# The scan of a two-layer hybrid backbone: the triangular inverse in whole steps, decay products on 64 rows each, copies on other engines

## The chip, the cores and the metric

The kernel runs on one core of a Trainium2 chip, as one program. The metric is device microseconds of one execution; before the change three executions took 2302.88, 2305.74 and 2308.2 us, median 2305.74.

The core has a TensorE (matmuls; "PE", with weight loads as "PEld"), VectorE ("DVE"), ScalarE ("ACT"), GpSimd ("POOL") and SyncE ("SP", which here issues nearly all DMAs). Each engine works through its own instructions in the order in which the program holds them, and waits on semaphores for the others.

## The reference

Two layers on 512 latent tokens and 256 context tokens of 1024 features, in float32: attention and a SwiGLU feed-forward, then a bidirectional RWKV-7 mixer and another feed-forward. The change touches only the mixer's scan, for 16 heads of 64 features in both directions:

```python
decay = exp(-exp(-softplus(-(w0[d] + tanh(xw @ w1[d]) @ w2[d])) - 0.5))
a     = sigmoid(a0[d] + (xa @ a1[d]) @ a2[d])
k_d   = k * (1 + (a - 1) * k_a)
...
def step(S, inp):                  # one token
    w_t, k_t, v_t, kk_t, a_t = inp[:5]
    sa = einsum('bhvk,bhk->bhv', S, -kk_t)
    S = S * w_t + sa[..., None] * (kk_t * a_t) + v_t[..., None] * k_t
    y = einsum('bhvk,bhk->bhv', S, r_t)
```

The scan runs over the context first, then over the latents, forwards for d = 0 and backwards for d = 1; the two y are added. The rank-64 matrices `rwkv_w2` and `rwkv_a2` (2 directions, 64 by 1024) give decays and rates.

## The kernel before

**The scan in chunks.** The kernel takes 64 tokens (a chunk) at a time. Inside a chunk the recurrence becomes a unit triangular system, whose inverse is worked out once; between chunks only the state S is carried. A *stage* is a pass p (the context, then the latents in two halves) over eight heads g of both directions, four chunks each. There are six stages. What stage s + 1 needs is made while stage s runs: four feature tiles by `elem` (with `front` for the next tile), then one `invert`.

**`front` (L1014 to L1036)** loads a tile's `kk` and the weights `wa` (L1022, four DMAs of 64 by 128), multiplies them with `t1` and `ta` (the tanh and linear inner products of both directions, 64 rows each, so 128 partitions hold both) and applies tanh on ScalarE (L1029, L1030), a scaling on GpSimd (L1033) and a running sum on VectorE (L1035). `wa` is one buffer of [128, 2, 2, 128], zeroed once: direction d fills its own 64 rows of `wa[:, d, x]`, the other 64 stay zero, and the product at L1028 runs over all 128 rows. Its result `z` (one bank, tag "z") is for one direction at a time.

**`elem` (L1038 to L1117)** makes from that the decayed keys and queries (`BK` at L1078 and L1079, `AR` and `GA`, for latents `R` at L1083), the bonus (L1084 to L1093), and the products inside the chunks (L1102 to L1107), which ScalarE copies into `GA` (masked by GpSimd, L1111) and into `AB`, the blocks to be inverted (L1115, L1116).

**`invert` (L1120 to L1181)** inverts 128 unit triangular blocks of 32 by 32, one on a partition, by forward substitution on VectorE: after a 32 by 32 transpose (L1123) and a mask (L1124, GpSimd), step s (1 to 30) adds to the rows below s, n = 31 - s of them, the multiple E[row, s] of row s, m = s columns. For m up to 3 (L1132) and n up to 3 (L1137) it goes by single fused instructions. For the 24 steps between, the rows are split into two halves: the outer product of either half (L1144, into `tmp`, a part of `O2`), then the sum of either half (L1147). Two transposes follow (L1150, L1151), TensorE merges pairs of blocks (L1162, L1176, L1178; results in a bank of tag "mg"), and ScalarE and VectorE copy the parts to `Xs` (L1168 on VectorE: the upper left blocks; L1169, L1181 on ScalarE).

**`scan` (L1211 to L1288)**, four chunks of a stage: S is the decayed state (L1226, VectorE); its halves are copied into `Tt` (L1227 on ScalarE, L1228 on VectorE, from the upper to the lower 64 partitions); `Bt` is a transpose (L1234, L1235); for latents `Rb` is filled from `R`, of either head by four copies (L1240: h = 0 on VectorE, h = 1 on ScalarE), and multiplied and masked into `GR` (L1244, L1245). Then come the products `pp` (L1252), copied to `Pb` (L1253 ScalarE, L1254 VectorE), `pu` with the inverse (L1258), copied to `Tt` (L1260, L1261), `pn` (L1267) and the new state `Sn` (L1272), and for latents `py` (L1281, L1282).

**The order of the work.** A planner sets it when the program is built: it takes each engine's instructions by the order of the program text as a priority, as soon as its own model has their inputs and buffers ready. The result is a fixed list for each engine. In the text a stage's `scan` stands first, then the next stage's four `elem`, then `invert`. Beside the first tiles run the products for v (L1197 to L1199), beside the context's stages those for r (L1308).

Of the kernel before, what the change touches and what calls it, by code (L numbers as in the profile page):

```python
# [10 lines left out]
F32 = mybir.dt.float32  # L11
# [6 lines left out]
P = 128  # L18
# [4 lines left out]
T = L + C  # L23
# [14 lines left out]
def tile_hybrid_backbone(ctx: ExitStack, tc: tile.TileContext, a: dict, out: bass.AP, dbg=None, stop=None, start=None):  # L38
# [32 lines left out]
    # ---- parameters, feature by feature on the partitions  # L71
# [44 lines left out]
    # ---- adaLN modulation: one block of 512 columns of mod_w  # L116
# [34 lines left out]
    # ---- the activation table of a function, loaded once x is there and before the function's first use  # L151
# [3 lines left out]
    # ---- 1 / sqrt(sum / n + eps), refined by a Newton step  # L155
# [11 lines left out]
    # ---- the sum of squares of the tokens sl, partition by partition, but for the last feature tile, whose squares follow  # L167
# [13 lines left out]
    # ---- the reciprocal root mean squares of nt tiles of tokens, tokens on the partitions  # L181
# [9 lines left out]
    # ---- the same on every partition, of the tokens dg has room for  # L191
# [7 lines left out]
    # ---- scale and shift of normed tokens  # L199
# [8 lines left out]
    # ---- a block of weights [nk * 128, cols], as the exact sum of two float32r parts  # L208
# [13 lines left out]
    # ---- out[f, t] += sum_d W[d, f] X[d, t] in three float32r passes; of several products all at once, step by step  # L222
# [10 lines left out]
    # ---- 512 columns of weights, as the exact sum of two float32r parts  # L233
# [19 lines left out]
    # ---- a product added to xT by its streams' gates  # L253
# [9 lines left out]
    # ---- xT += gate * (W^T X); the last tiles by halves of the tokens  # L263
# [23 lines left out]
    # The gate and up products of a pair of feature tiles by Winograd's form of Strassen's seven: the weights  # L287
    # A (features, d) and the tokens B (d, tokens) in 2 x 2 blocks,
    #   S1 = A21 + A22, S2 = S1 - A11, S3 = A11 - A21, S4 = A12 - S2
    #   T1 = B12 - B11, T2 = B22 - T1, T3 = B22 - B12, T4 = B21 - T2  # L290
    #   P1 = A11 B11, P2 = A12 B21, P3 = S4 B22, P4 = A22 T4, P5 = S1 T1, P6 = S2 T2, P7 = S3 T3
    #   C11 = P1 + P2, C12 = P1 + P6 + P5 + P3, C21 = P1 + P6 + P7 + P4, C22 = P1 + P6 + P7 + P5
    # Every sum is float32, every product three float32r passes.
    ORDER = (1, 2, 5, 6, 7, 3, 4)

    # ---- modulated norm of xT, in its place, as the blocks B11, B21, B22, T1 .. T4, each the exact sum of two float32r parts
# [51 lines left out]
    # ---- SwiGLU of the normed blocks, gated into xT; the hidden features in pairs of tiles  # L348
# [112 lines left out]
    # ================= x and ctx, features on the partitions  # L461
# [30 lines left out]
    # ---- layer 1's modulated norm of a stream, in its place  # L492
# [14 lines left out]
    # ================= layer 0: attention  # L507
    def layer0():
        at = ExitStack()
        with ExitStack() as qs:  # L510
# [43 lines left out]
            # rotary tables with the gains folded in; a head's features as (half, axis, pair)  # L554
# [27 lines left out]
            # heads' features onto the partitions; a pair of token tiles behind the products  # L582
# [151 lines left out]
        # ================= layer 0: projection and feed-forward  # L734
# [44 lines left out]
    # ================= layer 1: the RWKV mixer  # L779
# [7 lines left out]
    with ExitStack() as rw:  # L787
# [37 lines left out]
        with ExitStack() as de:  # L825
# [17 lines left out]
            # neighbours' sum, and the first lerp of it  # L843
# [57 lines left out]
            # the latents' second half again before their first, so that either pass reads one run  # L901
# [14 lines left out]
            # of a feature tile its heads, and the heads' features again from the two parts of a value  # L916
# [63 lines left out]
        # The scan's passes: the context, then the latents in two halves (each direction starts at its own  # L980
        # end). A stage is a pass over eight heads of both directions, 4 chunks of 64 tokens each. What a
        # stage needs of decays, keys and queries is worked out beside the stage before it.
# [10 lines left out]
        was = [tm.tile([P, 2, 2, P], F32, name=f"wa{z}") for z in range(1)]  # L993
        for z in Xss + was + ARs:
            nc.gpsimd.memset(z, 0.0)
# [7 lines left out]
        # a tile's decays begin before what is left of the tile before it  # L1003
# [10 lines left out]
        def front(p, f):  # L1014
# [4 lines left out]
            wa = was[0]  # L1019
            for x, nm_ in enumerate(("rwkv_w2", "rwkv_a2")):  # L1020
                for d in range(2):
                    nc.sync.dma_start(out=wa[hid(d), d, x], in_=a[nm_][0, d, :, P * f:P * f + P])  # L1022
            lw = tm.tile([P, 2, 256], F32, name="lw", tag="lw", bufs=2)
            at = tm.tile([P, 2, 256], F32, name="at", tag="at", bufs=2)
            for d in range(2):
                z = pE.tile([P, 2, 256], F32, name="z", tag="z")
                for x, src in enumerate((t1, ta)):
                    nc.tensor.matmul(z[:, x], wa[:, d, x], src[:, T0(p, d):T0(p, d) + 256], start=True, stop=True)  # L1028
                nc.scalar.activation(lw[:, d], z[:, 0], AF.Tanh, bias=hw0[:, d, f:f + 1], scale=0.5)  # L1029
                nc.scalar.activation(at[:, d], z[:, 1], AF.Tanh, bias=ha0[:, d, f:f + 1], scale=-0.5)  # L1030
# [7 lines left out]
        def elem(p, f):  # L1038
# [55 lines left out]
            # the products within the chunks; of the reverse direction's own the transposes  # L1094
# [24 lines left out]
        # unit triangular inverses, 128 blocks of 32 x 32 at a time, one on a partition, then merged in pairs  # L1119
        def invert():  # L1120
# [6 lines left out]
            tmp = O2.rearrange("p i b -> p (i b)")[:, 0:256]  # L1127
            for s in range(1, 31):
# [11 lines left out]
                h = (n + 1) // 2  # L1140
                parts = ((s + 1, s + 1 + h, 0), (s + 1 + h, 32, h * m))
                tvs = [tmp[:, o:o + (b - a_) * m].rearrange("p (a b) -> p a b", b=m) for a_, b, o in parts]
                for (a_, b, _), tv in zip(parts, tvs):
                    nc.vector.tensor_tensor(out=tv, in0=E[:, a_:b, s:s + 1].to_broadcast([P, b - a_, m]),  # L1144
                                            in1=E[:, s:s + 1, :s].to_broadcast([P, b - a_, m]), op=ALU.mult)
                for (a_, b, _), tv in zip(parts, tvs):
                    nc.vector.tensor_tensor(out=E[:, a_:b, :s], in0=E[:, a_:b, :s], in1=tv, op=ALU.add)  # L1147
# [18 lines left out]
            for h in range(2):  # L1166
                for d, o in ((0, o1), (1, o2)):
                    nc.vector.tensor_copy(Xs[lo(h), :, d, :, 0:32], o[lo(h), :, d])  # L1168
                    nc.scalar.copy(Xs[hi(h), :, d, :, 32:64], o[hi(h), :, d])  # L1169
# [13 lines left out]
        # beside v, tokens on the partitions  # L1183
# [27 lines left out]
        def scan(p, g):  # L1211
            fs = [f_tiles[p, 4 * g + q] for q in range(4)]
            Xs = Xss[0]
            for i in range(4):
# [6 lines left out]
                if not first:  # L1221
# [6 lines left out]
                    nc.vector.tensor_copy(Tt[HS[0], :, :, 1], S[HS[1]])  # L1228
# [7 lines left out]
                if p:  # L1236
                    GR = slot_pool["B"].tile([P, 2, 4, 2, 64], F32, name="GR", tag="GR")
                    for f in range(4):
                        for h in range(2):
                            (nc.scalar.copy if h else nc.vector.tensor_copy)(slot_pool["Rb"][HS[h], h, :, f], fs[f][2][HS[h], i:8 - i:7 - 2 * i, :])  # L1240
# [49 lines left out]
        # beside the context's passes  # L1290
# [40 lines left out]
    # ================= layer 1: readout, projection and feed-forward of the latents, final norm  # L1331
# [134 lines left out]
```

## Time and profile before

| | |
|---|---|
| median of three runs | 2305.74 us |
| span of the profiled execution | 2302.6 us |
| scan, from the first `front` to the end of the last stage | about 1253 to 1826 us of the span |
| first inverse begins | 1314.7 us |
| last inverse's transposes end | 1765.1 us |

The profile is one execution. Engine rows give busy microseconds. In a row of a group stand line, engine, operation, output <- inputs, partitions x elements and the count; behind the first bar the busy time and the mean of one in ns, behind the second the idle time of the engine just before them and what ended it. In a row of one line or tile the three numbers are minimum, median and maximum in ns. In a timeline row stand the start, the length, the engine and the line; "x2" is two neighbours merged. A window's row has the window, its length, then busy time and count for PE, PEld, DVE, ACT and POOL, the granted share of TensorE's clock, the DMA engines' share and GB/s. The chain of waits is followed back from the last instruction; its "by line" gives shares of the window.

### The profile page before, as it was taken

The numbers are of one execution on the slowest core, as the hardware profiler recorded it, in microseconds if no ns is written. First come the engines' busy times: TensorE is split into PE (matmuls) and PEld (weight loads), VectorE is DVE, ScalarE is ACT, GpSimd is POOL, SyncE is SP. The second block draws the span as 40 slices with busy tenths as digits, with TensorE's granted clock in tenths as the row PEclk, the third lists the DMA queues.
The fourth block names the chain that finished last, engine by engine and source line by source line (L and its number), as shares of the span: only waits on it lengthen the run. The fifth ranks groups of instructions, "written<-read, shape, count | busy, mean of one in ns | idle before, by whom it ended". The sixth has DMA issues, their size and how long they took to land.

```text
span 2302.6 us, 42745 instructions
## 1 busy us (share of the span) xinstructions
PE 2034.6 (88%) x16422; PEld 1779.6 (77%) x16422; DVE 1669.9 (73%) x3382; ACT 1094.9 (48%) x2276; POOL 790.8 (34%) x663
## 2 busy tenths in 40 slices
PE   6999999797999999995988978767888777899998
PEld 4995555586999999994767956656777666899998
DVE  4565556449877777768465597798888758988896
ACT  5446656434333333335343764765664534444443
POOL 1110000027434443423142531552430325666661
PEclk7999999998999999997988979778889987999999
DMA  8206660421321222111326543432321631433332
GB/s 298 67 25 222 237 237 21 148 91 48 109 74 63 74 68 74 62 55 64 100 88 211 148 121 120 121 107 64 110 62 54 189 121 47 138 97 97 105 97 74
DMA packets 178714, 247.94 MB, mean 108 GB/s; under 512 B 16808, under 2 KB 109968, under 8 KB 178128
## 3 DMA queue, kind: packets, MB, share of 16 engines
q1 hardware_dynamic: 177792, 244.37, 33.0%
q8 instruction: 130, 2.13, 0.4%
q10 hardware_dynamic: 352, 0.60, 0.1%
q0 software_dynamic: 368, 0.26, 0.1%
q14 instruction: 72, 0.59, 0.1%
HBM read 199.04 MB, written 33.55 MB: 101 GB/s over the span
## 4 chain that ended last, share of the span: by engine, by line
PE 63%; DVE 20%; ACT 5%; issue 5%; DMA 4%; POOL 2%; SPq 1%; DVEq 0%; ACTq 0%; POOLq 0%
PE yps L429 13%; PE A L395 8%; PE C L395 5%; PE B L395 5%; PE yps L228 5%; PE po L724 3%; DVE O L1144 3%; PE pj L228 3%; PE S L705 2%; DVE E L1147 2%; PE PTp L719 2%; PE mps L126 2%; DVE wu L241 2%; PE qps L578 2%; PE qps L580 2%
## 5 line engine op out<-in xcount | busy, mean ns | idle before, releaser
L429 PE MATMUL yps<-gh,wu 128*128 128x384 f32 (+2 forms) x1120 | 323.4, 345 | 3.7 <-DVE xT L258 3.6
L258 DVE SCALAR_TENSOR_TENSOR xT<-yps,modT,xT 128x384 f32<-128x384 f32 (+2 forms) x348 | 183.9, 548 | 134.1 <-PE yps L429 95.0
L241 POOL TENSOR_TENSOR wu<-wr,wu 128x512 fp32r<-128x512 f32 x77 | 107.1, 1392 | 472.6 <-ACT wu L239 456.9
L239 ACT CAST wu<-wr 128x512 fp32r<-128x512 f32 x252 | 154.6, 620 | 222.2 <-PE A L395 66.4
L429 PEld LDWEIGHTS yps<-gh,wu 128*128 128x128 f32 x1120 | 201.6, 188 | 16.5 <-DVE xT L258 4.7
L239 ACT CAST wu<-ws 128x512 fp32r<-128x512 f32 x176 | 108.0, 620 | 200.2 <-PE yps L429 86.5
L241 DVE TENSOR_TENSOR wu<-wr,wu 128x512 fp32r<-128x512 f32 x175 | 157.7, 903 | 50.8 <-ACT wu L239 47.8
L429 PE MATMUL yps<-gl,wu 128*128 128x384 f32 (+2 forms) x560 | 192.1, 344 | 0.0
L360 POOL TENSOR_TENSOR ws<-wr 128x512 f32<-128x512 f32 x88 | 130.1, 1482 | 165.8 <-DMA wr<-in_ffn_wg_dram 71.5
L241 DVE TENSOR_TENSOR wu<-ws,wu 128x512 fp32r<-128x512 f32 x111 | 125.8, 1139 | 9.8 <-ACT wu L239 9.8
L241 POOL TENSOR_TENSOR wu<-ws,wu 128x512 fp32r<-128x512 f32 x65 | 88.1, 1356 | 90.3 <-ACT wu L239 87.6
L429 PEld LDWEIGHTS yps<-gl,wu 128*128 128x128 f32 x560 | 105.4, 188 | 4.5
L228 PE MATMUL yps<-oTh,wu 128*128 128x512 f32 (+2 forms) x416 | 101.6, 347 | 8.2 <-ACT wu L239 8.2
L708 DVE TENSOR_REDUCE mx<-S 128x1 f32<-128x768 f32 (+1 forms) x96 | 74.7, 778 | 44.4 <-PE S L705 43.7
L720 ACT COPY PT<-PTp 128x384 f32<-128x384 f32 (+1 forms) x160 | 69.3, 465 | 54.0 <-PE PTp L719 53.8
L395 PE MATMUL C<-x5h,wu 128*128 128x384 f32 (+1 forms) x352 | 85.6, 318 | 6.0 <-ACT x5h L329 5.2
L719 PEld LDWEIGHTS PTp<-ident,pr 128*128 128x128 f32 x448 | 50.2, 144 | 50.5 <-issue 23.6
L395 PE MATMUL A<-x1h,wu 128*128 128x384 f32 (+1 forms) x352 | 88.0, 315 | 1.1 <-ACT x1h L329 1.1
L395 PE MATMUL B<-x2h,wu 128*128 128x384 f32 (+1 forms) x352 | 83.8, 310 | 4.7 <-ACT x2h L329 4.6
L1147 DVE TENSOR_TENSOR E<-E,O 128x110 f32<-128x110 f32 (+22 forms) x288 | 84.2, 325 | 0.3
L395 PE MATMUL A<-x6h,wu 128*128 128x384 f32 (+1 forms) x352 | 83.1, 314 | 1.0 <-DVE wu L241 1.0
L1144 DVE TENSOR_TENSOR O<-E 128x110 f32<-128x110 f32 (+22 forms) x288 | 82.4, 322 | 1.9
(408 smaller groups left out, 6365.4 us busy)
## 6 DMA issues: line engine op xcount, KB each, us to landing
mw<-in_mod_w_dram SPq DMA_DIRECT2D x48, 1024.0 KB, 5.3
wr<-in_ffn_wg_dram SPq DMA_DIRECT2D x44, 512.0 KB, 3.8
wr<-in_ffn_wu_dram SPq DMA_DIRECT2D x44, 512.0 KB, 3.6
wr<-in_ffn_wd_dram SPq DMA_DIRECT2D x44, 512.0 KB, 3.9
wraw<-in_rwkv_wrkv_dram SPq DMA_DIRECT2D x32, 256.0 KB, 3.1
wraw<-in_attn_wqkv_dram SPq DMA_DIRECT2D x12, 512.0 KB, 4.5
xT<-xd SPq DMA_DIRECT2D x2, 3072.0 KB, 9.8
AR<-lw SPq DMA_DIRECT2D x48, 128.0 KB, 2.3
```

Of the source, the lines that this page charges most:

```text
L228: nc.tensor.matmul(ps, w(k), x(k, sl), start=(k == 0 and i == 0), stop=(k == nk - 1 and i == 2))
L239: nc.scalar.copy(hi, raw)
L241: (nc.gpsimd if lane["n"] % 3 == 0 else nc.vector).tensor_tensor(out=lo, in0=raw, in1=hi, op=ALU.subtract)
L258: nc.vector.scalar_tensor_tensor(out=xT[:, f, t0:t1], in0=ps[:, t0 - sl.start:t1 - sl.start], scalar=modT[:, l, 8 * m + f, s:s + 1], in1=x ...
L360: nc.gpsimd.tensor_tensor(out=t, in0=x, in1=y, op=op)
L395: nc.tensor.matmul(ps, w[:, k], x[:, k], start=(k + j == 0), stop=(k == 3 and j == 2))
L429: nc.tensor.matmul(ps, u[k // 2][w][:, k % 2, fs], gs[k // 2][x][:, k % 2, sl], start=(k + j == 0), stop=(k == nk - 1 and j == 2))
L708: nc.vector.tensor_reduce(out=mx, in_=S[:, :nk * P], axis=AX.X, op=ALU.max)
L719: nc.tensor.transpose(ps[:, t - t0, :], pr_[:, P * t:P * t + P], ident)
L720: nc.scalar.copy(PT[h][:, t0:t1, P * qt:P * qt + P], ps[:, :t1 - t0, :])
L1144: nc.vector.tensor_tensor(out=tv, in0=E[:, a_:b, s:s + 1].to_broadcast([P, b - a_, m]), in1=E[:, s:s + 1, :s].to_broadcast([P, b - a_, m]) ...
L1147: nc.vector.tensor_tensor(out=E[:, a_:b, :s], in0=E[:, a_:b, :s], in1=tv, op=ALU.add)
```

## The change

Four edits, all in the scan, and a few comments less in the text.

- `front`: `wa` becomes a tile of [128, 2, 128] with two buffers, loaded by two DMAs of 128 rows; nothing is zeroed. Direction d's product takes only its own 64 rows of weights and of `t1` or `ta`. Both directions' results are open at once, one in the bank "z", the other in the bank "mg", and their products alternate.
- `invert`: each of the 24 middle steps is one outer product and one sum over all n rows.
- `invert`: the upper left blocks go to `Xs` on GpSimd instead of VectorE.
- `scan`: the second half of `Tt` comes from GpSimd instead of VectorE, and all eight `Rb` copies from ScalarE instead of four.

```diff
-        was = [tm.tile([P, 2, 2, P], F32, name=f"wa{z}") for z in range(1)]
-        for z in Xss + was + ARs:
+        for z in Xss + ARs:
...
-            wa = was[0]
+            wa = tm.tile([P, 2, P], F32, name="wa", tag="wa", bufs=2)
             for x, nm_ in enumerate(("rwkv_w2", "rwkv_a2")):
-                for d in range(2):
-                    nc.sync.dma_start(out=wa[hid(d), d, x], in_=a[nm_][0, d, :, P * f:P * f + P])
+                nc.sync.dma_start(out=wa[:, x], in_=a[nm_][0].rearrange("d k f -> (d k) f")[:, P * f:P * f + P])
...
+            zs = [pE.tile([P, 2, 256], F32, name="z", tag=t) for t in ("z", "mg")]
+            for x, src in enumerate((t1, ta)):
+                for d in range(2):
+                    nc.tensor.matmul(zs[d][:, x], wa[hid(d), x], src[hid(d), T0(p, d):T0(p, d) + 256], start=True, stop=True)
             for d in range(2):
-                z = pE.tile([P, 2, 256], F32, name="z", tag="z")
-                for x, src in enumerate((t1, ta)):
-                    nc.tensor.matmul(z[:, x], wa[:, d, x], src[:, T0(p, d):T0(p, d) + 256], start=True, stop=True)
+                z = zs[d]
...
-            tmp = O2.rearrange("p i b -> p (i b)")[:, 0:256]
+            tmp = O2.rearrange("p i b -> p (i b)")
...
-                h = (n + 1) // 2
-                parts = ((s + 1, s + 1 + h, 0), (s + 1 + h, 32, h * m))
-                tvs = [tmp[:, o:o + (b - a_) * m].rearrange("p (a b) -> p a b", b=m) for a_, b, o in parts]
-                for (a_, b, _), tv in zip(parts, tvs):
-                    nc.vector.tensor_tensor(out=tv, in0=E[:, a_:b, s:s + 1].to_broadcast([P, b - a_, m]),
-                                            in1=E[:, s:s + 1, :s].to_broadcast([P, b - a_, m]), op=ALU.mult)
-                for (a_, b, _), tv in zip(parts, tvs):
-                    nc.vector.tensor_tensor(out=E[:, a_:b, :s], in0=E[:, a_:b, :s], in1=tv, op=ALU.add)
+                tv = tmp[:, 0:n * m].rearrange("p (a b) -> p a b", b=m)
+                nc.vector.tensor_tensor(out=tv, in0=E[:, s + 1:, s:s + 1].to_broadcast([P, n, m]),
+                                        in1=E[:, s:s + 1, :s].to_broadcast([P, n, m]), op=ALU.mult)
+                nc.vector.tensor_tensor(out=E[:, s + 1:, :s], in0=E[:, s + 1:, :s], in1=tv, op=ALU.add)
...
-                    nc.vector.tensor_copy(Xs[lo(h), :, d, :, 0:32], o[lo(h), :, d])
+                    nc.gpsimd.tensor_copy(Xs[lo(h), :, d, :, 0:32], o[lo(h), :, d])
...
-                    nc.vector.tensor_copy(Tt[HS[0], :, :, 1], S[HS[1]])
+                    nc.gpsimd.tensor_copy(Tt[HS[0], :, :, 1], S[HS[1]])
...
-                            (nc.scalar.copy if h else nc.vector.tensor_copy)(slot_pool["Rb"][HS[h], h, :, f], fs[f][2][HS[h], i:8 - i:7 - 2 * i, :])
+                            nc.scalar.copy(slot_pool["Rb"][HS[h], h, :, f], fs[f][2][HS[h], i:8 - i:7 - 2 * i, :])
```

## The prediction

> **What bounds the kernel now.** I read the page first, then the chain of waits cut to the stretch that the edits touch, then the busy time of each engine by windows, and last the groups and single instructions of VectorE, TensorE and GpSimd.
>
> ```profile
> span 2302.6 us, 42745 instructions
> PE 2034.6 (88%) x16422; PEld 1779.6 (77%) x16422; DVE 1669.9 (73%) x3382; ACT 1094.9 (48%) x2276; POOL 790.8 (34%) x663
> by line: PE pv L1197 20.9%; PE pv L1199 20.6%; PE pv L1198 20.6%; PE z L1028 15.2%; PE A L1102 5.8%; DMA wraw<-in_rwkv_wrkv_dram 4.6%; DMA wa<-in_rwkv_w_dram 4.2%; PE A L1105 3.7%; DVE E L1123 3.2%; PE A L1107 2.9%; DVE wlo L219 1.1%; ACT w
> by line: DVE O L1144 13.2%; DVE E L1147 12.3%; PE pr L1308 7.6%; issue 4.9%; PE z L1028 3.9%; DVE lw L1035 2.4%; DVE BK L1078 2.3%; PE A L1244 2.1%; DVE E L1132 2.1%; DVE GR L1245 2.0%; PE A L1102 1.9%; DVE T L1228 1.8%; DVE Rb L1240 1.8%;
> 1315.00:1770.00 455.00, 357.86 (x5193) 297.85 (x5194) 394.05 (x1043) 266.17 (x593) 164.82 (x171) 0.84 0.34 98
> 1450.00:1500.00 50.00, 43.14 (x702) 36.59 (x700) 36.94 (x55) 40.62 (x89) 28.02 (x29) 0.77 0.45 125
> 1500.00:1560.00 60.00, 42.98 (x505) 35.60 (x504) 58.85 (x156) 36.71 (x83) 29.44 (x33) 0.78 0.35 101
> ```
>
> Over the whole span TensorE is busiest, but every edit lies in the scan, so the share of the span says little. The two lines "by line" are the chain in 1250 to 1315 us (products for v beside the first four tiles) and in 1315 to 1770 us (six inverses and five of the six scan stages). In the first, TensorE carries the chain. In the second the two lines of the inverse, L1144 and L1147, alone hold 25.5% of 455 us, 116 us, and the window row has VectorE at 394.05 of 455 us, ScalarE at 266.17, GpSimd at 164.82. The last two rows show that this alternates: while an inverse runs, VectorE has no room (58.85 of 60); between inverses, while the next stage's tiles are made, it has (36.94 of 50). Work taken off VectorE pays in the first kind of stretch only.
>
> **The change part by part.** Each term is microseconds of the chain; a minus is a gain.
>
> *The inverse in one piece.* It now has four VectorE instructions for a step (two products, two sums, the halves interleaved), 576 in all; afterwards two, 288, each with twice the elements.
>
> ```profile
> L1147 DVE TENSOR_TENSOR E<-E,O 128x110 f32<-128x110 f32 (+22 forms) x288 | 84.2, 325 | 0.3
> L1144 DVE TENSOR_TENSOR O<-E 128x110 f32<-128x110 f32 (+22 forms) x288 | 82.4, 322 | 1.9
> L1144 DVE TENSOR_TENSOR O<-E x288: 199/260/1327, 1321.0 to 1759.1; 128x110 f32<-128x110 f32 x18, 128x120 f32<-128x120 f32 x18, 128x78 f32<-128x78 f32 x12, 128x96 f32<-128x96 f32 x12
> 1532.89 0.26 DVE L1147 TENSOR_TENSOR E<-E,O 128x112 f32<-128x112 f32 x1
> 1533.07 0.46 DVE L1144 TENSOR_TENSOR O<-E 128x120 f32<-128x120 f32 x2
> 1533.46 0.46 DVE L1147 TENSOR_TENSOR E<-E,O 128x120 f32<-128x120 f32 x2
> 1533.95 0.48 DVE L1144 TENSOR_TENSOR O<-E 128x128 f32<-128x128 f32 x2
> 1534.35 0.47 DVE L1147 TENSOR_TENSOR E<-E,O 128x128 f32<-128x128 f32 x2
> 1534.73 0.47 DVE L1144 TENSOR_TENSOR O<-E 128x119 f32<-128x119 f32 x2
> 1609.44 0.68 DVE L1226 TENSOR_TENSOR S<-Sn,Ft 128x512 f32<-128x512 f32 x1
> ```
>
> An instruction of 112 elements takes 0.26 us and one of 512 takes 0.68, so 1.05 ns an element over 0.14 us fixed. Neighbours overlap by 0.08: the one at 1532.89 would end at 1533.15 and the next began at 1533.07. A step of 120 elements took 0.88 us (1533.07 to 1533.95), one of 128 took 0.78 (to 1534.73). The slower one held a wait: its last sum ended at 1533.92, and the next product began 0.03 us after that end instead of 0.08 before it. That is the price of an instruction that needs the result just ahead of it, 0.11 us, and the halves hide most of it. In one piece both instructions of a step need the one ahead: each is 0.14 + 240 × 1.05 ns = 0.39 us, plus 0.03 if nothing lies between, 0.85 a step, or 0.39 − 0.08 each, 0.63 a step, where other work lies between. With a third of the gaps filled, my choice because in the windows above other VectorE work is mixed into the inverses, a step costs 0.78 against 0.83 now. Over 6 × 24 = 144 steps that saves 7 us of VectorE; the chain holds 116 of the 166.6 us of these lines, 0.70, so **−5**. The ends: all filled, −20 (144 × 0.20 × 0.70); none filled and the cheap 0.78 us as what it has now, +7.
>
> Here the Trainium skill (VectorE: DVE Perf Modes, "The DRAIN you can't avoid") has a rule for a larger gain: every instruction must empty the pipeline before the next starts, and a semaphore costs nothing extra. The rows above differ: independent neighbours overlap by 0.08 us and only a dependent one waits. (The page adds that an instruction not held starts earlier.) By the rule the two halves hide nothing, and the time it gives is among the rivals.
>
> *Copies.* L1228 (one half of T, 22 times) and the upper-left blocks of Xs at L1168 (24 times) go from VectorE to GpSimd, half of the Rb copies at L1240 (64) to ScalarE.
>
> ```profile
> L1240 DVE COPY Rb<-R 64x128 f32<-64x128 f32 x64 | 18.6, 302 | 4.5 <-POOL R L1083 2.4 <-PE py L1282 1.8
> L1228 DVE COPY T<-S 64x512 f32<-64x512 f32 x22 | 13.0, 598 | 0.6
> L1168 DVE COPY Xs<-O 32x512 f32<-32x512 f32 x12 | 6.9, 573 | 0.0
> L1168 DVE COPY Xs<-AB 32x512 f32<-32x512 f32 x12 | 5.2, 433 | 2.9 <-PE pu L1258 2.8
> L1240 ACT COPY Rb<-R 64x128 f32<-64x128 f32 x48 | 12.4, 293 | 3.5 <-POOL R L1083 2.0 <-PE py L1282 0.9
> L1111 POOL TENSOR_SCALAR_AFFINE_SELECT GA<-GA 64x512 f32<-64x512 f32 x40 | 33.1, 827 | 82.4 <-ACT GA L1109 81.1
> L1033 POOL TENSOR_SCALAR lw<-lw 128x256 f32<-128x256 f32 x38 | 18.3, 481 | 50.8 <-ACT lw L1029 43.4 <-DVE O L1144 5.4 <-DVE E L1137 0.9
> 1611.29 1.30 DVE L1240 COPY Rb<-R 64x128 f32<-64x128 f32 x1
> 1612.62 1.31 DVE L1228 COPY T<-S 64x512 f32<-64x512 f32 x1
> ```
>
> VectorE loses 18.6 + 13.0 + 12.1 = 44 us. On the chain of 1315 to 1770 L1240 and L1228 have 1.8% each, 8 us each; L1168 is not named there. L1240: 8 us go; ScalarE takes 64 more at 0.293, 19 us on top of its 266 in 455, queued in the scan step ahead of the evictions Bt, Pb and T of later steps; with ScalarE 58% busy I charge 3, so **−5** (ends −8 and +4). L1228: no row shows this copy on GpSimd. Nearest from below is the 0.60 of VectorE, from above the 0.83 of the select on the same 64 × 512; I take 0.8, nearer the row of the same engine. Against that, VectorE often comes to it late: S was ready at 1610.12 (1609.44 + 0.68) and the copy began at 1612.62, behind an Rb copy among others. GpSimd, busy 36% of the time, would mostly begin at once; the recurrence is then about as late as now, but VectorE is free for the inverse: **−4** of the 8 (the ends are −8 and the first rival). L1168 follows the last transposes of an inverse, where VectorE has room and four ScalarE copies run beside it: **−1** (ends −4 and +4).
>
> *What the copies take back.* GpSimd gets 46 copies at about 0.75, 34 us, and VectorE waits for GpSimd where both read SBUF:
>
> ```profile
> 1321.01 1.41 DVE L1144 TENSOR_TENSOR O<-E 128x56 f32<-128x56 f32 x2
> 1322.34 1.66 DVE L1147 TENSOR_TENSOR E<-E,O 128x56 f32<-128x56 f32 x2
> 1321.03 2.53 POOL L1301 TENSOR_TENSOR rl<-rl,rh 128x512 fp32r<-128x512 f32 x2
> ```
>
> Four instructions of 56 elements lasted 3.0 us beside two GpSimd subtractions that ended at 1323.56. This is why the mean of L1144 is 322 ns and its median 260: about 63 ns × 576 = 36 us of waiting in the inverses, 0.22 us for each us of GpSimd's 164.82. For 34 more that is 7.5 of VectorE, × 0.70, **+5** (ends 0 and, if each copy stops VectorE throughout, +24). The Trainium skill (SBUF — State Buffer, "Who interferes with whom") calls it an exclusive lock on a shared port pair; these rows agree.
>
> *Decay products.* The weights `wa` were zero-padded to 128 rows for each direction; now either direction has its own 64 rows and its own bank, and the two are issued in turn. The program's fp32 product stands in the trace as two matmuls.
>
> ```profile
> L1028 PE MATMUL z<-t,wa 128*128 128x256 f32 x96 | 39.0, 495 | 4.6 <-DMA wa<-in_rwkv_w_dram 2.6 <-ACT at L1030 1.9
> 1276.15 0.59 PE L1028 MATMUL z<-t,wa 128*128 128x256 f32 x2
> 1276.58 0.59 PE L1028 MATMUL z<-ta,wa 128*128 128x256 f32 x2
> 1400.41 0.70 PE L1028 MATMUL z<-t,wa 128*128 128x256 f32 x2
> 1401.04 1.09 PE L1258 MATMUL pu<-Pb,Xs 128*64 128x128 f32 x14
> SPq L1022 <- PE z L1028: 44.8, 28, 5.2
> L1022 SPq DMA_DIRECT2D wa<-in_rwkv_w_dram x48: 465/488/578, 1252.8 to 1653.0; - x48
> ```
>
> Two take 0.43 us (1276.15 to 1276.58), a tile's eight 1.72. z holds 15.2% of 65 us and 3.9% of 455 us of the chain, 27.6 us. No row has two products on separate rows. The nearest are the 14 pu products on separate column halves: 14 × 0.108 us (half of 0.215, 128 of 256 columns) is 1.51, and they took 1.09, of which some 0.16 is the last one's tail (as in z's pair, 0.59 − 0.43): 1.6 times as fast. That would take 10 from 27.6. A change of shape costs: after 128*64 products the first pair of z took 0.70 instead of 0.59, so two changes for each of 24 tiles are 5 us, of which the chain would hold a third as it does of z (27.6 of twice 39.0). In the first window the products for v follow at once on a full TensorE, later ScalarE's tanh is next late; I keep **−5** (ends −14, a full pairing, and +2, none). The Trainium skill (TensorEngine Tiling, "Key Properties") says a change of tiling mode drains the engine; the 0.70 agrees in kind.
>
> The `wa` loads fall from 96 to 48 issues of about 0.49 us on SyncE's queue, and with two buffers they no longer wait for the products before (44.8 us of queue time, with loads of the same queue behind them, but mostly early enough): **−1** (ends −6 and 0). The second bank of z is the one that the inverse's merges use: the next tile's front can wait for their evictions, six times, and the wait of the second direction for ScalarE (1.9 us) goes: **+1** (ends −1 and +6).
>
> **Sum**: −5 −5 −4 −1 +5 −5 −1 +1 = −15 us. The profiled span 2302.6 becomes 2287.6; the median of the runs lies 3.1 us above that span, so 2290.7, **2291 us**.
>
> **The rivals.**
> *GpSimd's order holds up the recurrence (slower).* The T copy stands between S and the next products, and GpSimd works strictly in its written order. If the copy is written behind an instruction that waits, it waits too: L1111 waited 82.4 us in 40, L1033 50.8 in 38, about 2 and 1.3 us each. Half of the 22 copies behind such a wait plus its 0.83 is 11 × 2.9 = 32 us, × 0.63 (8.2 of 13.0 us of L1228 are on the chain) = 20, and the 4 of L1228 are lost: 2302.6 − 15 + 24 = 2311.6, 2315 us. It decides from about 20 us of delay, 0.9 us for each copy. Against it: GpSimd idles 64% here.
> *Nothing to measure.* The one-piece steps stay unfilled (+5 instead of −5) and the row halves don't pair (0 instead of −5): 2302.6 us, 2306. For it: the halves already hide what one piece exposes.
> *The whole pipeline flush counts.* If each instruction costs its full length whatever follows, 288 fewer save 0.14 + 0.03 each, 49 us, × 0.70 = 34 instead of 5: 2262 us. The overlap of 0.08 speaks against it.
>
> **How the numbers follow.** Forecast 0.56, slower rival 0.22, no change 0.16, flush 0.06. A difference under 0.2%, 4.6 us, can't be told from none. The terms' ends pull the forecast to either side by some 15 us; the range reaches from 2267, short of the flush case, to 2315, the slower rival. Faster 0.62, same 0.16, slower 0.22; the forecast's own range is 2276 to 2300.
>
> **What would show it.** Right: VectorE's busy time in the scan falls by 35 to 50 us; steps of the inverse follow at 0.65 to 0.85 us; z of both directions begins at nearly the same time; the chain still has L1144 and L1147's successors in front, with ScalarE and GpSimd larger. Wrong: GpSimd's T copy appears as what TensorE's pp products wait for, with microseconds between S and its start; ScalarE above 70% with Bt or Pb behind Rb copies; or steps at 0.9 us and more, with a larger gap between mean and median.

## The result and the profile after

The changed kernel takes 2386.62 us (median of four, 2380.86 to 2388.92), the kernel before 2306.24 us on the same chip: ratio 1.0341, 95% interval 1.0318 to 1.0365. The forecast was 2291 with a range of 2267 to 2315, so it erred in sign and far in size: the change costs 80 us.

Three lines of the page after; the third has, behind its second bar, the idle time of TensorE just ahead of the merge products and what ended it:

```profile
span 2387.2 us, 42299 instructions
PE 2047.7 (86%) x16422; PEld 1784.2 (75%) x16422; DVE 1615.1 (68%) x2984; ACT 1112.3 (47%) x2340; POOL 818.2 (34%) x708
L1159 PE MATMUL mg<-O,AB 32*32 32x32 f32 x768 | 21.6, 229 | 97.1 <-DVE O L1147 85.5
```

No engine got much more to do (TensorE 13 us more, VectorE 55 us less), and yet TensorE stood idle for 85.5 us until the first of the inverse's two closing transposes (L1147) let the merges begin. Where that lies is seen from the six inverses: the transpose that begins each (E<-AB) and the second of the two that end it (AB<-E), with the start of the first and of the last. Before, then after:

```profile
L1123 DVE STREAM_TRANSPOSE E<-AB x6: 1927/1972/2040, 1314.7 to 1727.2; 128x1024 f32<-128x1024 f32 x6
L1151 DVE STREAM_TRANSPOSE AB<-E x6: 1874/1898/1940, 1373.4 to 1763.3; 128x1024 f32<-128x1024 f32 x6
```

```profile
L1124 DVE STREAM_TRANSPOSE E<-AB x6: 1901/1968/2044, 1314.9 to 1826.6; 128x1024 f32<-128x1024 f32 x6
L1148 DVE STREAM_TRANSPOSE AB<-E x6: 1871/1878/1904, 1358.2 to 1855.4; 128x1024 f32<-128x1024 f32 x6
```

The first inverse begins at the same time. Then one follows the other every 102.3 us ((1826.6 − 1314.9) / 5) instead of every 82.5. Yet the first and the last inverse themselves are shorter, 43.3 and 28.8 us between these transposes instead of 58.7 and 36.1. The last transpose comes 92.1 us later, and what follows it is 7.5 us shorter (2387.2 − 1855.4 against 2302.6 − 1763.3): 84.6, the whole difference of the spans. So the loss lies between the inverses.

Busy time by windows after (PE, PEld, DVE, ACT, POOL, then the clock): the second inverse up to its merges, what follows, the third inverse, what follows, and the whole stretch:

```profile
1430.00:1462.00 32.00, 12.42 (x185) 10.62 (x184) 28.15 (x69) 8.50 (x20) 3.83 (x6) 0.66 0.08 25
1462.00:1529.00 67.00, 53.64 (x695) 43.98 (x690) 29.67 (x45) 41.44 (x91) 34.32 (x37) 0.60 0.34 96
1529.00:1560.00 31.00, 11.77 (x155) 10.68 (x157) 28.46 (x70) 6.75 (x17) 4.17 (x5) 0.72 0.06 18
1560.00:1629.00 69.00, 56.20 (x957) 46.53 (x957) 35.93 (x52) 48.88 (x113) 35.24 (x38) 0.85 0.38 105
1315.00:1870.00 555.00, 384.49 (x5601) 317.66 (x5601) 348.71 (x673) 291.52 (x667) 194.59 (x215) 0.78 0.29 84
```

An inverse now runs nearly alone (the third): VectorE 28.46 of 31 us, TensorE 11.77, ScalarE 6.75, GpSimd 4.17. In the prediction's row for 1500 to 1560 us, inside an inverse of before, the three had 42.98, 36.71 and 29.44 of 60. What used to run beside the inverse now runs behind it, in stretches of 67 and 69 us. The granted clock was 0.60 in the one and 0.85 in the other, but the two hold different work (695 and 957 matmuls), so the clock's share in their length can't be read from these rows.

The waits in 1310 to 1860 us after (line, what it waited for, us in total, times, longest), and the first TensorE rows behind the second inverse:

```profile
POOL Xs L1165 <- DVE O L1147: 115.5, 6, 25.5
...
ACT Xs L1166 <- DVE O L1147: 88.9, 6, 25.2
PEld mg L1159 <- DVE O L1147: 87.4, 6, 22.0
PE mg L1159 <- DVE O L1147: 85.5, 5, 21.6
```

```profile
1461.74 1.92 PE L1159 MATMUL mg<-O,AB 32*32 32x32 f32 x64 [14.90 <-DVE O L1147]
...
1472.30 1.92 PE L1175 MATMUL mg<-W,AB 32*32 32x32 f32 x64 [1.26 <-ACT Xs L1178]
...
1477.38 1.22 PE L1027 MATMUL z<-t,wa 64*128 64x256 f32 x2
1478.40 1.06 PE L1027 MATMUL z<-ta,wa 64*128 64x256 f32 x2
```

GpSimd, ScalarE and TensorE stand still until the inverse is done, 15 to 19 us a time on average. The next tile's decay products (L1027) come behind the last merge.

### The profile page after: what moved, and what is told of

The parts are those of the page before. It is cut to its first block, busy times and chain, and to the rows that moved or that the text cites. A ratio compares the mean times of both kernels' runs of the same rounds, so it can differ in the third digit from the quotient of the medians.

```text
span 2387.2 us, 42299 instructions
## 1 busy us (share of the span) xinstructions
PE 2047.7 (86%) x16422; PEld 1784.2 (75%) x16422; DVE 1615.1 (68%) x2984; ACT 1112.3 (47%) x2340; POOL 818.2 (34%) x708
## 5 line engine op out<-in xcount | busy, mean ns | idle before, releaser
L241 DVE TENSOR_TENSOR wu<-wr,wu 128x512 fp32r<-128x512 f32 x175 | 145.4, 833 | 48.6 <-ACT wu L239 45.8
L1159 PE MATMUL mg<-O,AB 32*32 32x32 f32 x768 | 21.6, 229 | 97.1 <-DVE O L1147 85.5
L1159 PEld LDWEIGHTS mg<-O,AB 32*32 32x32 f32 x768 | 20.0, 144 | 100.0 <-DVE O L1147 87.4
L395 PE MATMUL C<-x5h,wu 128*128 128x384 f32 (+1 forms) x352 | 85.5, 317 | 7.2 <-ACT x5h L329 4.9
L395 PE MATMUL B<-x7h,wu 128*128 128x384 f32 (+1 forms) x352 | 83.1, 318 | 1.5 <-ACT x7h L329 1.5
```

Of the source, the lines that this page charges most:

```text
L241: (nc.gpsimd if lane["n"] % 3 == 0 else nc.vector).tensor_tensor(out=lo, in0=raw, in1=hi, op=ALU.subtract)
L395: nc.tensor.matmul(ps, w[:, k], x[:, k], start=(k + j == 0), stop=(k == 3 and j == 2))
```

## The experiments

**The theory and its rivals.** In the text `invert` stands between the `front` of the next stage's first tile and that of its second, since an `elem` calls the `front` of the tile after it. The second direction's z now asks for the bank "mg", of which there is one. In this program a bank goes round in the order of the text, so the second to fourth tile of the next stage, whole, cannot begin before the merges have had the bank, and the merges come at the end of the inverse. Rivals: the 64-row products or their loads are themselves dear; the one-piece steps or the copies on GpSimd and ScalarE are; or the planner's new order of everything is, whatever the edit.

**The bank: three kernels.** `e1_one_bank` is the changed kernel with both directions in bank "z", one after the other:

```diff
-            zs = [pE.tile([P, 2, 256], F32, name="z", tag=t) for t in ("z", "mg")]
-            for x, src in enumerate((t1, ta)):
-                for d in range(2):
-                    nc.tensor.matmul(zs[d][:, x], ...)
             for d in range(2):
-                z = zs[d]
+                z = pE.tile([P, 2, 256], F32, name="z", tag="z")
+                for x, src in enumerate((t1, ta)):
+                    nc.tensor.matmul(z[:, x], wa[hid(d), x], src[hid(d), ...], ...)
```

> The changed kernel, but the two directions' decay products again go one after the other through the one bank z (on 64 rows still); one-piece inverse and copies stay as changed. Bank theory (a front that needs the merges' bank stands in the text behind the inverse's merges, so no work of the next tiles can run beside an inverse): 2285 to 2310 us, decay products between the start of an inverse and its merges again, no wait of 20 us of TensorE for the inverse's transpose. Copies theory (the T copy on GpSimd and the Rb copies on ScalarE delay the recurrence): stays at 2370 to 2390 us. One-piece theory (the steps in one piece leave no room for other work): stays at 2370 to 2390 us too.

`e2_second_bank` is the kernel before with one edit, the bank of the second direction:

```diff
-                z = pE.tile([P, 2, 256], F32, name="z", tag="z")
+                z = pE.tile([P, 2, 256], F32, name="z", tag=("z", "mg")[d])
```

> The kernel before, with one thing changed: the second direction's decay products go to the merges' bank mg. Weights padded to 128 rows, halved inverse and all copies as before. Bank theory: slow by itself, 2370 to 2400 us, with TensorE, ScalarE and GpSimd idle some 20 us in each inverse. Copies and one-piece theories: 2295 to 2312 us, as before.

`e3_merge_in_A` is the changed kernel with the merges' results in the two banks "A":

```diff
-                ps = pE.tile([P, 16, 32], F32, name="mg", tag="mg")
+                ps = pE.tile([P, 16, 32], F32, name="mg", tag="A", bufs=2)
-                ps = pE.tile([P, 4, 4, 32], F32, name="mg2", tag="mg")
+                ps = pE.tile([P, 4, 4, 32], F32, name="mg2", tag="A", bufs=2)
```

> The changed kernel, with the inverse's merges moved to the two banks A of the scan's transposes, so that the bank mg holds nothing but the second direction's decay products. Bank theory: the overlap comes back and the pairs of products stay, 2275 to 2305 us; if what matters is any bank between an inverse and later work, the scan's transposes are now behind the merges, which costs little as the scan waits for the inverse anyway. Copies and one-piece theories: 2370 to 2390 us.

Measured against 2304.94 of before: e1 2323.73 (1.0087, 1.0072 to 1.0102), **e2 2390.83** (1.0385, 1.0359 to 1.0411), e3 2318.66 (1.0061, 1.0043 to 1.008). The one line of e2 makes the whole loss, 86 us, and taking the shared bank out of the changed kernel gives back, by the ratios, 59 (e1: 1.0087 against 1.0341) or 65 (e3: 1.0061). The inverses, a window inside one and a wait of e2, then the inverses of e3:

```profile
L1123 DVE STREAM_TRANSPOSE E<-AB x6: 1904/1960/2039, 1320.9 to 1831.4; 128x1024 f32<-128x1024 f32 x6
L1151 DVE STREAM_TRANSPOSE AB<-E x6: 1866/1880/1914, 1364.6 to 1858.2; 128x1024 f32<-128x1024 f32 x6
```

```profile
1531.00:1561.00 30.00, 8.61 (x146) 7.85 (x144) 28.86 (x118) 6.62 (x16) 4.27 (x7) 0.67 0.07 20
```

```profile
PE mg L1162 <- DVE O L1150: 103.2, 6, 27.2
```

```profile
L1124 DVE STREAM_TRANSPOSE E<-AB x6: 1944/1966/2037, 1314.4 to 1754.0; 128x1024 f32<-128x1024 f32 x6
L1148 DVE STREAM_TRANSPOSE AB<-E x6: 1893/1928/1955, 1372.4 to 1793.2; 128x1024 f32<-128x1024 f32 x6
```

e2 keeps the steps in halves, the padded weights and the old copies, and has the period of after, 102.1 us, and its empty inverses (TensorE 8.61 of 30). In e3 the period is 87.9. This settles the main cause. It leaves 14 to 19 us: e1 and e3 are still slower than before, and both lie above the range that the bank theory had set for them.

**The other parts one by one.** `e4_one_piece` is the kernel before with the one-piece steps alone:

> The kernel before with the inverse's steps in one piece, nothing else. Bank theory: no slow-down from it; by my price of the steps 2300 us (5 us less), within 2286 to 2313. One-piece theory: most of the loss, 2350 us or more, with inverses that run alone. If every VectorE instruction cost its full length whatever follows: 2270 us.

Measured 2304.89, 0.9999 (0.9985 to 1.0013): nothing, within 3.5 us. `e5_T_on_gpsimd` has only the T copy moved, `e6_Rb_on_scalar` only the Rb copies:

```diff
-                    nc.vector.tensor_copy(Tt[HS[0], :, :, 1], S[HS[1]])
+                    nc.gpsimd.tensor_copy(Tt[HS[0], :, :, 1], S[HS[1]])
```

```diff
-                            (nc.scalar.copy if h else nc.vector.tensor_copy)(slot_pool["Rb"][HS[h], h, :, f], ...)
+                            nc.scalar.copy(slot_pool["Rb"][HS[h], h, :, f], ...)
```

> The kernel before with one thing changed: the second half of T is copied by GpSimd (22 copies). The kernel with one bank for the decay products stayed 19 us slower than before, with GpSimd waiting 50 us at this copy for S. Queue theory (the copy stands at the head of GpSimd's queue and waits for S, and the next tiles' work behind it starts late): 8 to 20 us slower, 2313 to 2325. Price of the prediction (VectorE freed, GpSimd mostly idle): 2297 to 2305. If the loss sits in the other copies or in the 64-row products: 2302 to 2308.

> The kernel before with one thing changed: all eight Rb copies of a chunk on ScalarE. Theory that ScalarE's queue then delays Bt, Pb and T: 5 to 15 us slower, 2310 to 2320. Price of the prediction: 5 us faster, 2300, between 2297 and 2309. If the loss is GpSimd's T copy alone: within 4 us of before.

Against 2307.34: e5 2312.78 (1.0027, 1.0014 to 1.0039), e6 2320.48 (1.0063, 1.0047 to 1.0078). `e7_rows64_one_bank` has the weights in two unpadded buffers by two loads and the products on 64 rows, in the one bank "z"; `e8_pairs_own_bank` the decay products wholly as changed, with the merges in banks "A":

```diff
...
-            wa = was[0]
+            wa = tm.tile([P, 2, P], F32, name="wa", tag="wa", bufs=2)
...
-                for d in range(2):
-                    nc.sync.dma_start(out=wa[hid(d), d, x], in_=a[nm_][0, d, :, P * f:P * f + P])
+                nc.sync.dma_start(out=wa[:, x], in_=a[nm_][0].rearrange("d k f -> (d k) f")[:, P * f:P * f + P])
...
-                    nc.tensor.matmul(z[:, x], wa[:, d, x], src[:, ...], ...)
+                    nc.tensor.matmul(z[:, x], wa[hid(d), x], src[hid(d), ...], ...)
```

> The kernel before with the weights wa in two unpadded buffers and 64-row products, both directions one after the other in the one bank z. Queue and ScalarE theories: no cost here, 2298 to 2308. If the 64-row shape itself costs (changes of the array's shape around each group, no pairing): 3 to 8 us slower, 2309 to 2314. Load theory (fewer issues and a second buffer relieve SyncE's queue): 2295 to 2302.

> The kernel before with the decay products as changed (64 rows each, two banks, alternating) and the inverse's merges moved to the banks A; halved steps and all copies as before. If pairing pays as priced: 5 to 10 us faster, 2295 to 2300. If the scan's transposes behind the merges cost as much: 2302 to 2312. If the bank alone accounts for the whole loss and the copies for nothing, this equals the run that changed all but the bank, 2314 to 2321.

e7 2334.79 (1.0122, 1.0103 to 1.014), e8 2332.52 (1.0113, 1.0095 to 1.0132), both above every range set for them. So with no bank shared the kernels with the new decay products are 25 to 27 us slower. Four more kernels were to find out by what. `e9_shape_only`: the padded buffer and four loads as before, the product on its own 64 rows. `e10_full_rows`: e7 with products over all 128 rows (each then adds the other direction's product; the work is the same). `e11_one_wa_buffer`: e7 with one buffer. `e12_merges_in_A_only`: before with the merges in banks "A".

```diff
# e9, on before
-                    nc.tensor.matmul(z[:, x], wa[:, d, x], src[:, ...], ...)
+                    nc.tensor.matmul(z[:, x], wa[hid(d), d, x], src[hid(d), ...], ...)
# e10, on e7
-                    nc.tensor.matmul(z[:, x], wa[hid(d), x], src[hid(d), ...], ...)
+                    nc.tensor.matmul(z[:, x], wa[:, x], src[:, ...], ...)
# e11, on e7
-            wa = tm.tile([P, 2, P], F32, name="wa", tag="wa", bufs=2)
+            wa = tm.tile([P, 2, P], F32, name="wa", tag="wa", bufs=1)
```

> The kernel before (one padded buffer wa, its four loads, one bank), but each decay product uses only its direction's 64 rows. The kernel with 64-row products and the two unpadded buffers was 27 us slower, with TensorE's granted clock at 0.79 in the scan against 0.84. Shape theory (64-row products cost by themselves, by changes of shape or by a lower granted clock): most of the 27 us is here, 2318 to 2335, clock 0.80 or less. Load theory (the two-buffered loads change the planned order of SyncE's queue and so of the rest): 2300 to 2312, clock 0.83 or more.

> The counterpart: the two unpadded buffers and two loads a tile of the change, one bank z, but each product runs over all 128 rows. It then adds both directions' products, so decays and rates differ from the reference's; the amount of work is the same. Shape theory: as fast as before, 2300 to 2312. Load theory: as slow as with 64 rows, 2325 to 2340.

> 64-row products, one bank, two loads a tile, but one buffer wa instead of two. Load theory, by the second buffer: back to 2300 to 2312. Load theory, by the form of the loads alone, or shape theory: 2320 to 2338.

> The kernel before with only the inverse's merges moved from the bank mg to the two banks A. It tells what the cure of the bank costs by itself: if the scan's transposes behind the merges cost nothing, 2298 to 2310; if that is why the pairs in banks of their own were 25 us slower than before, 2315 to 2335.

Against 2307.77: e9 2312.08 (1.0023, 1.0006 to 1.004), e10 2319.69 (1.0054, 1.0035 to 1.0073), e11 2331.32 (1.0106, 1.0081 to 1.013), e12 2320.98 (1.006, 1.0039 to 1.0082). None of them isolates the loss: every small edit costs 4 to 24 us, even e12, which only moves results between banks.

**The planner's order by itself.** So I measured edits that change no work (neutral edits). `e13_loads_swapped` asks for the two decay weights in the other order, `e14_pb_swapped` swaps the two Pb copies in the text, `e15_both_swapped` does both. `e16_without_products` is the kernel before with the one-piece steps and all the moved copies, and the decay products as before.

```diff
# e13, on before
-            for x, nm_ in enumerate(("rwkv_w2", "rwkv_a2")):
+            for x, nm_ in ((1, "rwkv_a2"), (0, "rwkv_w2")):
```

> The kernel before with a neutral edit: the two halves of wa are loaded in the other order (rwkv_a2 first). No instruction is added, removed, moved to another engine or made longer, only the planner's order of the scan changes (hundreds of places on each engine). If each single edit's loss is its own cost (shape, loads, merges in A, Rb on ScalarE): 2303 to 2311, as before. If a good part of it is the plan, which any edit reshuffles away from a favourable one: 2312 to 2330.

> A second neutral edit of the kernel before: the two copies of Pb, on different engines, stand in the other order in the text. Own costs: 2303 to 2311. Plan: anywhere from 2300 to 2330, and different from the other neutral edits.

> Both neutral edits together, a third plan for the same work. Own costs: 2303 to 2311. Plan: not the sum of the two alone.

> The change without its decay products: one-piece steps, the upper left blocks of Xs and the T copy on GpSimd, all Rb copies on ScalarE; loads, weights and the bank of z as before. Own costs that add up: T on GpSimd 6, Rb on ScalarE 14, the steps 0, 2325 to 2332 us. Copies that free VectorE as the prediction had it: 2292 to 2300. Plan: 2300 to 2325, not the sum.

Against 2305.17: e13 2297.76 (0.9972, 0.9959 to 0.9985), e14 2312.97 (1.0028, 1.0012 to 1.0043), e15 2323.56 (1.0079, 1.0057 to 1.0102), e16 2297.93 (0.9968, 0.9955 to 0.998). The same work in another order costs −7, +8 or +18 us, so a difference of some 20 us or less between two of these kernels can't be put down to the edit: it may be the order's. e16 is faster than both kernels, though e4, e5 and e6 came to +18 together. The last two kernels put the same neutral edits on e16: `e17_copies_loads_swapped` and `e18_copies_pb_swapped`.

> The kernel without the new products (2297.93 us in the last study, 0.9968) with the two decay weights loaded in the other order, an edit that changes no work and that moved the kernel before by -7 us. If the 7 us that the copies and the one-piece steps gained are their own, this gives 2290 to 2304 us. If they come from the order of instructions that the planner happened on, it gives anything from 2290 to 2325, and with the next kernel a spread of over 12 us.

> The kernel without the new products, with the two Pb copies of a chunk in the other order of text, an edit that changes no work and that moved the kernel before by +8 us. If the 7 us are the copies' own: 2294 to 2304 us, within 6 us of the kernel with the loads swapped. If they are the plan's: one of the two is above 2306 us.

Against 2307.04: e17 2299.66 (0.9969, 0.9957 to 0.998), e18 2309.29 (1.0013, 1.0003 to 1.0023). By the mark set beforehand, one above 2306 us, the gain of e16 may be the order's as much as its own. With the same swap on both sides, the steps and copies gain 7.2 us (e16 against before), nothing (0.9969 and 0.9972) and 3.5 us (1.0013 and 1.0028).

**Where the order's share lies.** The traces tell more than the totals. From the start of the first inverse to that of the transpose that ends the last one, before takes 448.6 us (1763.3 − 1314.7). The same two rows of e15, of e9 (the shape alone) and of e10 (the loads alone):

```profile
L1123 DVE STREAM_TRANSPOSE E<-AB x6: 1892/1958/2048, 1311.5 to 1731.7; 128x1024 f32<-128x1024 f32 x6
L1151 DVE STREAM_TRANSPOSE AB<-E x6: 1868/1890/1948, 1369.5 to 1765.6; 128x1024 f32<-128x1024 f32 x6
```

```profile
L1123 DVE STREAM_TRANSPOSE E<-AB x6: 1899/1943/2039, 1323.0 to 1734.4; 128x1024 f32<-128x1024 f32 x6
L1151 DVE STREAM_TRANSPOSE AB<-E x6: 1868/1940/2002, 1378.5 to 1772.4; 128x1024 f32<-128x1024 f32 x6
```

```profile
L1121 DVE STREAM_TRANSPOSE E<-AB x6: 1933/1986/2046, 1310.8 to 1744.2; 128x1024 f32<-128x1024 f32 x6
L1149 DVE STREAM_TRANSPOSE AB<-E x6: 1861/1885/1911, 1369.2 to 1782.0; 128x1024 f32<-128x1024 f32 x6
```

In this stretch the neutral edits differ from before by 8 us at most (450.1, 455.9 and 454.1 in e13 to e15); most of e15's +18 lies behind it, where e15 takes 554.3 us and before 539.3. The shape alone costs nothing here (e9, 449.4 us), the loads alone 23 (e10, 471.2), both 30 (e7, 479.0). The six kernels with the new loads and no shared bank (e1, e3, e7, e8, e10, e11) take 463 to 489 us, the twelve without the new loads (before and the others but e2) 442 to 460. So the new loads, two of 128 rows into unpadded buffers, go with a longer stretch, by more than the neutral edits scatter there. The gap is thin at its edge, though: e12, which only moves a bank, takes 460.3, e11 463.1. Each figure is of one profiled execution, and which wait makes the difference isn't shown.

## Why the prediction was wrong, point by point

**The step that failed** is the last term, "The second bank of z is the one that the inverse's merges use: the next tile's front can wait for their evictions, six times, and the wait of the second direction for ScalarE (1.9 us) goes: **+1** (ends −1 and +6)." The place and the waiter were right, and the count nearly (five of the six inverses are followed by another stage's tiles); the length was not: +1 stood against 86 us measured, and the end of +6 was no bound. The term priced the wait by an eviction, as if the bank came free as soon as asked for. It comes free when the merges have had their turn, and their turn comes after an inverse. The 86 us are e2's, which has this edit and no other. The prediction's own row for 1500 to 1560 us had the warning: TensorE, ScalarE and GpSimd with 43, 37 and 29 us of work inside an inverse, work that the bank now puts behind it. The Trainium skill (Perfetto Trace Analysis, "Matmuls") advises independent products to rotate through different PSUM banks, so that the eviction of one overlaps the next. Here e2 shows where that ends: the bank added to the rotation had a user with a longer turn.

The other terms, at their own size:

*One piece.* Predicted −5 (−20 to +7), e4 gives 0. The steps of the third inverse after:

```profile
1545.02 0.41 DVE L1142 TENSOR_TENSOR O<-E 128x238 f32<-128x238 f32 x1
1545.46 0.41 DVE L1144 TENSOR_TENSOR E<-E,O 128x238 f32<-128x238 f32 x1
1545.91 0.41 DVE L1142 TENSOR_TENSOR O<-E 128x240 f32<-128x240 f32 x1
```

An instruction took 0.41 us (0.39 predicted) and the next began 0.03 after its end, as predicted: 0.89 a step (1545.02 to 1545.91) where the unfilled step was put at 0.85. In halves it was 0.83, so undisturbed steps would lose 0.06 × 144 × 0.70 = 6 us, near the end of +7. e4 shows neither this loss nor the −5, but both are smaller than what the order alone scatters, so the term's sign stays open; what e4 excludes is a large gain. In e4 the busy time of the two lines falls from 166.6 to 134.2 us and the time not at all:

```profile
L1141 DVE TENSOR_TENSOR O<-E 128x108 f32<-128x108 f32 (+7 forms) x144 | 67.7, 470 | 3.1
L1143 DVE TENSOR_TENSOR E<-E,O 128x108 f32<-128x108 f32 (+7 forms) x144 | 66.5, 462 | 3.0
```

Where instructions of the two lines overlap, the sum of the lines counts the overlap twice. VectorE's own busy time in 1315 to 1770 us, which counts it once, falls by only 13 us (394.05 to 380.64). What the chain pays is the time from one step to the next.

*Copies.* The prices of the single copies held. Groups of after in 1250 to 1920 us:

```profile
L1237 ACT COPY Rb<-R 64x128 f32<-64x128 f32 x128 | 37.9, 296 | 2.4
L1249 PE MATMUL pp<-T,GA 128*64 128x64 f32 (+1 forms) x768 | 42.9, 256 | 2.6 <-DMA T<-d_v 2.3 <-POOL T L1225 0.3
L1225 POOL COPY T<-S 64x512 f32<-64x512 f32 x22 | 16.7, 764 | 18.7 <-DVE S L1223 18.0
```

T on GpSimd took 0.76 us (0.8 predicted), Rb on ScalarE 0.296 (0.293). VectorE's busy time in the scan fell by 45 us (394.05 to 348.71), inside the predicted 35 to 50; in e16, where the other engines work beside the inverses again, by 31 (to 362.92 below), short of it. Steps, copies and what GpSimd's copies cost VectorE were to give −5 −5 −4 −1 +5 = −10 together; e16 gives −7, and 0 and −3.5 in the other two orders. None of the three reaches −10. The sign is likely, the size not settled. e16 in the scan:

```profile
1315.00:1775.00 460.00, 368.77 (x5563) 307.42 (x5562) 362.92 (x673) 292.18 (x667) 191.66 (x215) 0.86 0.35 100
```

*Decay products.* Predicted −5 (−14 to +2) and −1 for the loads; with no bank shared, e7 and e8 give +27 and +25 on before, and e1 and e3 stand 27 and 21 above e16 (1.0087 and 1.0061 against 0.9968). Where the two directions' products come together, they do better than predicted and pair fully. Eight matmuls of e3, then four of before, both where two in a row of the same direction take some 1.2 us:

```profile
1442.84 1.23 PE L1027 MATMUL z<-t,wa 64*128 64x256 f32 x4
1443.85 1.07 PE L1027 MATMUL z<-ta,wa 64*128 64x256 f32 x4
```

```profile
1454.01 1.22 PE L1028 MATMUL z<-t,wa 128*128 128x256 f32 x2
1455.03 1.06 PE L1028 MATMUL z<-ta,wa 128*128 128x256 f32 x2
```

Eight matmuls end 2.08 us after the first began (1443.85 + 1.07 − 1442.84), as four did before (1455.03 + 1.06 − 1454.01). The Trainium skill (TensorEngine Tiling (Array Packing), "Key Properties") states that tiles work independently of each other, and these rows agree. But the directions come together in only 12 of e3's 24 tiles. In the changed kernel as it was measured they often don't: the row behind its second inverse above (1477.38) has two matmuls in 1.22 us, as before. In e3 z takes less time than before, so z is not where its 21 us go. In all four comparisons the loss is above the largest neutral edit, but not by much, and the neutral edits themselves lie up to 26 us apart (e13 and e15). What supports a loss of its own is the stretch between the inverses: 30 us in e7, where the neutral edits scatter by 8, nothing in e9 and 23 in e10. So it goes with the new loads and their buffers rather than with the 64-row shape, and the term of −1 for the loads is the one in doubt; through which wait they would cost so much is open. The granted clock doesn't decide it: over that stretch it was 0.78 to 0.82 in e1, e3, e7 and e8, 0.84 in before, and 0.82 in e14 and e15, which change no work. Whether a lower clock follows from the slower order or causes it wasn't told apart.

*The rivals.* GpSimd's order didn't hold up the recurrence: TensorE's pp waited 0.3 us in all for GpSimd's T. Rather the copy stood early in GpSimd's list and GpSimd waited in front of it for S, 18.0 us. The slower side came from another mechanism than my rival of that sign. That the steps gain nothing, half of the rival "nothing to measure", fits e4 (this rival puts the unfilled steps at +5, where their own term ends at +7). The pipeline flush would have shown in e4 as a gain of 34 us, more than any order scattered; there is none. So the rule of the Trainium skill that the prediction weighed (VectorE: DVE Perf Modes, "The DRAIN you can't avoid") does not describe the halves, which overlapped.

## What to carry to other kernels

Before you give a result a bank or buffer that exists once, list who else asks for it, in the order of the program, and ask when that other user gets its turn: the price is all the work between the two requests that used to overlap, not the other user's eviction. A window in which one engine is busy alone for 30 us, with the others at 4 to 12, is the mark of it, and moving one of the two users to another bank is the test. Where a planner sets the order of everything, time a few edits that change no work first: what they scatter is the least that an edit must gain to be believed. And look at the stretch that the edit touches, not only at the total: here the order's scatter was 8 us in that stretch and up to 26 in all.

## What the runs showed of the hardware and the program that was not expected

- Products on separate row halves in separate banks overlapped completely where they came together (four in 1.23 us in e3, as two in 1.22 before). In all, with half of the tiles paired, z took 27.5 + 24.0 us in e3 against 42.0 + 36.1 in e1, where the same 64-row products follow each other in one bank.

```profile
L1027 PE MATMUL z<-t,wa 64*128 64x256 f32 x96 | 27.5, 506 | 3.7 <-ACT at L1031 2.0 <-DMA wa<-in_rwkv_w_dram 1.7
L1027 PE MATMUL z<-ta,wa 64*128 64x256 f32 x96 | 24.0, 436 | 0.0
```

```profile
L1027 PE MATMUL z<-t,wa 64*128 64x256 f32 x96 | 42.0, 524 | 3.6 <-DMA wa<-in_rwkv_w_dram 2.0 <-ACT at L1029 1.6
L1027 PE MATMUL z<-ta,wa 64*128 64x256 f32 x96 | 36.1, 464 | 0.0
```

- Edits that change no work move this kernel by −7 to +18 us, and such effects don't add up: −7 and +8 gave +18 together.
